# Mixer weights split once inside two feed-forward stages and kept in DRAM, and rotary tables built in the third

## The chip, the cores and the metric

The kernel runs on one core of one Trainium2 chip. The metric is the device time in microseconds (us) of one execution; lower is better. Five engines work side by side: PE (TensorE, matrix products), DVE (VectorE), ACT (ScalarE), POOL (GpSimd) and SP (SyncE, which here only issues transfers). Each takes its own instructions in order and waits for others by semaphores. Transfers between DRAM and the on-chip memory run on 16 shared DMA engines.

## What is computed

A two-layer decoder trunk on 512 tokens of width 1024, all in float32. Each layer is a feed-forward with half weight, a mixer, and a second feed-forward with half weight, each behind an RMS norm and added to the residual. The first layer's mixer is a short gated convolution beside an RWKV-7 recurrence; the second's is a latent attention (MLA) with rotary position encoding. Cut from the reference:

```python
def _swiglu(h, w_gate, w_up, w_down):
    return (jax.nn.silu(h @ w_gate) * (h @ w_up)) @ w_down
...
def _conv_rwkv_mixer(h, w_in, conv_w, mu_shift, w0, w_up, a0, a_up, g_up,
                     k_k, k_a, r_k, ln_w, ln_b, w_out):
...
    p = h @ w_in
    p_conv, p_rwkv = p[..., :3 * CONV_WIDTH], p[..., 3 * CONV_WIDTH:]
...
    y_conv = gate_b * _short_conv(gate_c * h_in, conv_w)
...
    y = _rwkv7_scan(r_h, decay_h, k_h, v_h, -kk, kk * a_h)
...
    return jnp.concatenate([y_conv, y_rwkv], axis=-1) @ w_out
...
def _mla_mixer(h, cos, sin, w_in, q_a_norm, kv_a_norm, w_q_up, w_kv_up, q_norm, k_norm, w_out):
...
    c_q, c_kv, k_pe = jnp.split(p, (Q_RANK, Q_RANK + KV_RANK), axis=-1)
    q = (_rmsnorm(c_q, q_a_norm) @ w_q_up).reshape(B, T, MLA_HEADS, QK_DIM)
    kv = (_rmsnorm(c_kv, kv_a_norm) @ w_kv_up).reshape(B, T, MLA_HEADS, NOPE_DIM + V_DIM)
...
    q = jnp.concatenate([q[..., :NOPE_DIM], _rope(q[..., NOPE_DIM:], cos, sin)], axis=-1)
...
    o = _causal_attention(q, k, v)
    return o.reshape(B, T, MLA_HEADS * V_DIM) @ w_out
```

## The kernel before

The order of the stages is: first feed-forward (ffn 0), convolution and RWKV-7 mixer (`even`), second feed-forward (ffn 1), third feed-forward (ffn 2), latent attention (`mla`), fourth feed-forward (ffn 3). The activations `x` stay on chip as eight tiles of 128 x 512.

**Every product is done as three.** A float32 operand is cut into a high part, a copy rounded to the engine's faster format, and a low part, the remainder. `mm3` (L101 to L105) then multiplies high by high, high by low and low by high. The activations are cut once per stage (`xh`, `xl`, L120 and L121). The weights are cut each time they are used, in `weight` (L67 to L79): a transfer on SP brings a raw block of 128 x 512 (L72, tile `wr`, four buffers), ACT copies it into `wh` (L74), and DVE subtracts to get `wl` (L75); `wh` and `wl` have four buffers each. A caller may hand in `lo_on` to have POOL do the subtraction: the mixer does so for 64 of its 67 blocks (from `proj` and `proj_steps` at L731, the convolution's steps `even_conv` at L1029 and the output product `even_out` at L1081), and the attention's output product `mla_out` (L348) does so for all 16. The attention's input product `mla_in` (L364 to L374) cuts its own 16 blocks into the resident tiles `wih` and `wil`, with every second pair of subtractions on POOL.

**The feed-forward** (`ffn`, L161 to L192) runs 22 gate and up steps, each of two weights of 128 x 1024 (four blocks, 48 matrix instructions), with a SiLU and its own cut of the result behind them (L176 to L184), and then 8 down steps of 66 matrix instructions. Its argument `aside` is called once, in step 2: ffn 0 loads constants there, and ffn 2 builds the rotary tables (`rope_tables`: some forty small DVE instructions of 128 x 128, L244 to L300, and two sines on ACT), with their temporaries in a pool of their own.

**The mixer** interleaves the recurrence's long chains on DVE and ACT with products of the convolution as filler: `fill(n)` takes n steps of the generator `even_conv`, each one `mm3`.

**The order.** The program is written as one stream, and the framework's scheduler then orders each engine's instructions by a simulation of its own, under the dependencies and the buffers' reuse. So the tables of ffn 2 stand, in the order that results, already at the end of `even` and the start of ffn 1, where DVE has their turn. Transfers go round robin over eight slots, so that at most eight of SP's are under way.

## Time and profile before

| | us |
|---|---|
| median of 3 runs | 2032.48 (2031.89 to 2035.05) |
| profiled execution, its own time | 2034.76 |
| its span in the trace | 2032.8 |
| ffn 0 after its first step (24.4 to 373.0) | 348.60 |
| mixer (373.0 to 716.3) | 343.30 |
| ffn 1, first step (716.3 to 732.2) | 15.90 |
| ffn 1, the rest (732.2 to 1080.9) | 348.70 |
| ffn 2 (1080.9 to 1441.6) | 360.70 |
| latent attention (1441.6 to 1668.6) | 227.00 |
| ffn 3, first step (1668.6 to 1680.3) | 11.70 |
| ffn 3, the rest (1680.3 to 2032.0) | 351.70 |

The stretches are cut where PE begins the stage. A row of windows gives the length of a stretch and, for each engine, the microseconds in which it was busy and its number of instructions; then the granted clock of PE as a share of full speed, the mean busy share of the 16 DMA engines and what they moved. An engine busy for the whole stretch sets its length; where none is, the chain of waits and the rows of the single instructions tell who waited for whom.

### The profile page before, as it was taken

The numbers are of one execution on the slowest core, as the hardware profiler recorded it, in microseconds if no ns is written. First come the engines' busy times: TensorE is split into PE (matmuls) and PEld (weight loads), VectorE is DVE, ScalarE is ACT, GpSimd is POOL, SyncE is SP. The second block draws the span as 40 slices with busy tenths as digits, with TensorE's granted clock in tenths as the row PEclk, the third lists the DMA queues.
The fourth block names the chain that finished last, engine by engine and source line by source line (L and its number), as shares of the span: only waits on it lengthen the run. The fifth ranks groups of instructions, "written<-read, shape, count | busy, mean of one in ns | idle before, by whom it ended". The sixth has DMA issues, their size and how long they took to land.

```text
span 2032.8 us, 26989 instructions
## 1 busy us (share of the span) xinstructions
PE 1953.0 (96%) x10030; PEld 1593.5 (78%) x10030; DVE 1083.8 (53%) x1914; ACT 771.1 (38%) x1497; POOL 297.9 (15%) x342
## 2 busy tenths in 40 slices
PE   8999999967999999999999999999988999999999
PEld 6888888756776778888888888888877788888887
DVE  6444433599944874444335444433377775444422
ACT  5333333632422453333333333333475554333321
POOL 2000000266324410000000000000353430000000
PEclk9999999988999999999999999999998999999999
DMA  4222233221111123233333323333311123323332
GB/s 147 95 98 99 91 102 96 78 63 53 47 38 50 60 92 100 94 98 97 96 94 100 97 94 101 94 101 97 96 35 34 42 68 100 98 94 100 102 112 81
DMA packets 99892, 174.47 MB, mean 86 GB/s; under 512 B 11792, under 2 KB 20496, under 8 KB 99760
## 3 DMA queue, kind: packets, MB, share of 16 engines
q1 hardware_dynamic: 99760, 172.74, 27.3%
q8 instruction: 79, 1.29, 0.3%
q14 instruction: 53, 0.43, 0.1%
HBM read 170.60 MB, written 2.10 MB: 85 GB/s over the span
## 4 chain that ended last, share of the span: by engine, by line
PE 65%; DVE 9%; issue 2%; POOL 2%; ACT 2%; DMA 1%; POOLq 0%; ACTq 0%; DVEq 0%
PE po L103 7%; PE po L104 7%; PE po L105 7%; PE pu L103 6%; PE pu L104 6%; PE pu L105 6%; PE pg L104 6%; PE pg L103 6%; PE pg L105 6%; PE pp L103 1%; PE pp L104 1%; PE pp L105 1%; PE s L910 0%; DVE pr L935 0%; DVE ma L942 0%
## 5 line engine op out<-in xcount | busy, mean ns | idle before, releaser
L74 ACT ACTIVATE wh<-wr 128x512 fp32r<-128x512 f32 (+2 forms) x647 | 399.1, 619 | 905.2 <-PE pg L104 455.4
L75 DVE TENSOR_TENSOR wl<-wr,wh 128x512 fp32r<-128x512 f32 (+2 forms) x567 | 384.7, 682 | 413.9 <-ACT wh L74 413.3
L103 PE MATMUL pg<-xh,wh 128*128 128x512 f32 x704 | 276.8, 393 | 6.7 <-ACT wh L74 6.0
L103 PE MATMUL pu<-xh,wh 128*128 128x512 f32 x704 | 275.3, 391 | 3.3 <-DVE x L1088 2.6
L104 PE MATMUL pg<-xl,wh 128*128 128x512 f32 x704 | 275.5, 391 | 1.8 <-DVE xl L121 1.7
L105 PE MATMUL pg<-xh,wl 128*128 128x512 f32 x704 | 274.8, 390 | 0.0
L104 PE MATMUL pu<-xl,wh 128*128 128x512 f32 x704 | 274.8, 390 | 0.0
L105 PE MATMUL pu<-xh,wl 128*128 128x512 f32 x704 | 274.7, 390 | 0.0
L103 PE MATMUL po<-ah,wh 128*128 128x512 f32 x704 | 273.9, 389 | 0.0
L104 PE MATMUL po<-al,wh 128*128 128x512 f32 x704 | 273.9, 389 | 0.0
L105 PE MATMUL po<-ah,wl 128*128 128x512 f32 x704 | 273.9, 389 | 0.0
L176 DVE TENSOR_TENSOR g<-pg,rinv 128x512 f32<-128x512 f32 x88 | 60.9, 692 | 286.8 <-PE pg L105 286.4
L140 POOL TENSOR_TENSOR acc<-acc,sq 128x512 f32<-128x512 f32 x42 | 57.2, 1361 | 1050.9 <-ACT sq L139 1050.6
L103 PEld LDWEIGHTS pg<-xh,wh 128*128 128x128 f32 x704 | 132.7, 188 | 35.3 <-ACT wh L74 6.0
L104 PEld LDWEIGHTS pg<-xl,wh 128*128 128x128 f32 x704 | 132.7, 188 | 32.2 <-DVE xl L121 4.1
L103 PEld LDWEIGHTS pu<-xh,wh 128*128 128x128 f32 x704 | 132.6, 188 | 32.1 <-ACT sin L285 2.9
L105 PEld LDWEIGHTS pu<-xh,wl 128*128 128x128 f32 x704 | 132.6, 188 | 28.0 <-DVE wl L75 0.2
L105 PEld LDWEIGHTS pg<-xh,wl 128*128 128x128 f32 x704 | 132.7, 188 | 27.8 <-DVE wl L75 0.5
L104 PEld LDWEIGHTS pu<-xl,wh 128*128 128x128 f32 x704 | 132.7, 189 | 27.5
L104 PEld LDWEIGHTS po<-al,wh 128*128 128x128 f32 x704 | 132.1, 188 | 27.6
L105 PEld LDWEIGHTS po<-ah,wl 128*128 128x128 f32 x704 | 132.1, 188 | 27.5
L103 PEld LDWEIGHTS po<-ah,wh 128*128 128x128 f32 x704 | 132.1, 188 | 27.2
(365 smaller groups left out, 2641.8 us busy)
## 6 DMA issues: line engine op xcount, KB each, us to landing
wr<-in_wg SPq DMA_DIRECT2D x176, 256.0 KB, 2.5
wr<-in_wu SPq DMA_DIRECT2D x176, 256.0 KB, 2.8
wr<-in_wd SPq DMA_DIRECT2D x160, 256.0 KB, 2.6
wr<-in_w_ei SPq DMA_DIRECT2D x49, 256.0 KB, 2.6
wr<-in_wd SPq DMA_DIRECT2D x32, 128.0 KB, 2.0
wr<-in_w_eo SPq DMA_DIRECT2D x16, 256.0 KB, 2.5
wr<-in_w_oo SPq DMA_DIRECT2D x16, 256.0 KB, 3.0
wr<-in_w_q SPq DMA_DIRECT2D x12, 192.0 KB, 2.4
```

The lines of the kernel that those rows point to most:

```text
L74: nc.scalar.activation(hi, raw, AF.Copy)
L75: (lo_on or nc.vector).tensor_tensor(lo, raw, hi, op=ALU.subtract)
L103: nc.tensor.matmul(ps, wh, xh, start=first, stop=False)
L104: nc.tensor.matmul(ps, wh, xl, start=False, stop=False)
L105: nc.tensor.matmul(ps, wl, xh, start=False, stop=last)
L140: nc.gpsimd.tensor_tensor(acc, acc, sq, op=ALU.add)
L176: nc.vector.tensor_tensor(g, pg, rinv, op=ALU.mult)
```

## The change

In ffn 0 and ffn 1 a new generator, `presplit`, runs beside the gate, up and down steps. It takes the mixer's 67 blocks (17.43 MB, `even_blocks`) in ffn 0 and the attention's 52 blocks (11.53 MB, `mla_blocks`) in ffn 1, in 24 groups, one group per step from step 2 on. A block is loaded (tile `sr`, L113), copied by ACT into `sh` and subtracted by DVE into `sl` one step later, and both parts are sent to DRAM tiles `pre` (L100) a step after that. `weight` then no longer splits such a block: it issues two transfers, of the high part into `wh` (L77) and of the low part into `wl` (L78). `mla_in` does the same for `wih` and `wil` (L428). All POOL subtractions of weights are gone with it. The temporaries of the rotary tables are now in ffn 2's own pool. The on-chip area set aside for the program's DMA descriptors is set to 2048.

```diff
@@ -66,9 +68,15 @@
 
     def weight(self, src, cols, scale=None, lo_on=None):
         nc = self.nc
-        raw = self.wp.tile([128, WCOL], F32, name=self.uid("wr"), tag="wr", bufs=NRAW)[:, 0:cols]
+        raw = None
+        if not isinstance(src, tuple):
+            raw = self.wp.tile([128, WCOL], F32, name=self.uid("wr"), tag="wr", bufs=NRAW)[:, 0:cols]
         hi = self.wp.tile([128, WCOL], F32R, name=self.uid("wh"), tag="wh", bufs=NSPLIT)[:, 0:cols]
         lo = self.wp.tile([128, WCOL], F32R, name=self.uid("wl"), tag="wl", bufs=NSPLIT)[:, 0:cols]
+        if isinstance(src, tuple):
+            nc.sync.dma_start(hi.bitcast(F32), src[0])
+            nc.sync.dma_start(lo.bitcast(F32), src[1])
+            return hi, lo
         nc.sync.dma_start(raw, src)
         if scale is None:
             nc.scalar.activation(hi, raw, AF.Copy)
@@ -78,6 +86,34 @@
             nc.vector.scalar_tensor_tensor(lo, raw, scale, hi, op0=ALU.mult, op1=ALU.subtract)
         return hi, lo
 
+    def presplit(self, pool, groups):
...
+        nc = self.nc
+        tile_ = lambda tag, n, dt: pool.tile([128, WCOL], dt, name=self.uid(tag), tag=tag, bufs=6)[:, 0:n]
+        loaded, ready = [], []
+        for group in chain(groups, ((), ())):
+            for key, hi, lo in ready:
+                both = []
+                for a in (hi, lo):
+                    dst = self.dp.tile([128, a.shape[-1]], F32, name=self.uid("pre"))
+                    nc.sync.dma_start(dst, a.bitcast(F32))
+                    both.append(dst)
+                self.pre[key] = tuple(both)
+            ready = []
+            for key, raw in loaded:
+                n = raw.shape[-1]
+                hi, lo = tile_("sh", n, F32R), tile_("sl", n, F32R)
+                nc.scalar.activation(hi, raw, AF.Copy)
+                nc.vector.tensor_tensor(lo, raw, hi, op=ALU.subtract)
+                ready.append((key, hi, lo))
+            loaded = []
+            for key, src in group:
+                raw = tile_("sr", src.shape[-1], F32)
+                nc.sync.dma_start(raw, src)
+                loaded.append((key, raw))
+            yield
+
...
-    def ffn(self, j, y=None, aside=None):
+    def ffn(self, j, y=None, aside=None, later=()):
         tc, nc = self.tc, self.nc
+        later = list(later)
...
+            steps = NF + KD - 6 if later else 0
+            n = len(later)
+            split = self.presplit(ap, [later[n * i // steps : n * (i + 1) // steps] for i in range(steps)])
             for m in range(NF):
+                if m > 1:
+                    next(split, None)
...
                 if m == 2 and aside is not None:
-                    aside()
+                    aside(ap)
...
             for m in range(KD):
+                next(split, None)
...
-    def rope_tables(self, mp):
-        with self.tc.tile_pool(name="rope", bufs=1) as rp:
-            self.rope_build(rp, mp)
-
-    def rope_build(self, rp, mp):
-        nc = self.nc
-        t = lambda s: rp.tile([128, 4, 32], F32, name=self.uid(s))
-        pi = rp.tile([128, 4], mybir.dt.int32, name="posi")
+    def rope_tables(self, mp, ap):
+        nc = self.nc
+        a = ap.tile([128, 8 * T], F32, name="ropetmp", tag="ropetmp")
+        free = [a[:, i * 128 : i * 128 + 128] for i in range(28)]
+        t = lambda s: free.pop().rearrange("p (b f) -> p b f", b=4)
+        pi = ap.tile([128, 4], mybir.dt.int32, name="posi")
...
-        gn = rp.tile([128, 128], F32, name="gn")
+        gn = free.pop()
         nc.sync.dma_start(gn, self.d["rope_g"])
-        ng = rp.tile([128, 256], F32, name="ng")
+        ng = a[:, 28 * 128 : 30 * 128]
         nc.sync.dma_start(ng, self.d["nope_g"])
...
+    def mla_blocks(self):
+        d, out = self.d, []
+        for k in range(KD):
+            for c in (slice(0, 384), slice(384, 704)):
+                out.append((("w_oi", k, c.start), d["w_oi"][k][:, c]))
+        for hp in range(4):
+            for k in range(2):
+                out.append((("w_kv", hp, k), d["w_kv"][hp, :, k * 512 : k * 512 + 512]))
+            for k in range(3):
+                out.append((("w_q", hp, k), d["w_q"][hp, :, k * 384 : k * 384 + 384]))
+            for m in range(0, KD, 2):
+                out.append((("w_oo", hp, m), d["w_oo"][hp, :, m * 256 : m * 256 + 512]))
+        return out
...
         for m in range(0, KD, 2):
-            wh, wl = self.weight(self.d["w_oo"][hp, :, m * 256 : m * 256 + 512], 512, lo_on=nc.gpsimd)
+            wh, wl = self.weight(self.pre["w_oo", hp, m], 512)
...
             for c in (slice(0, 384), slice(384, 704)):
-                raw = self.wp.tile([128, WCOL], F32, name=self.uid("wr"), tag="wr", bufs=NRAW)[:, 0 : c.stop - c.start]
-                nc.sync.dma_start(raw, d["w_oi"][k][:, c])
-                nc.scalar.activation(h[:, c], raw, AF.Copy)
-                (nc.vector if k % 2 == 0 else nc.gpsimd).tensor_tensor(l[:, c], raw, h[:, c], op=ALU.subtract)
+                for dst, src in zip((h, l), self.pre["w_oi", k, c.start]):
+                    nc.sync.dma_start(dst[:, c].bitcast(F32), src)
...
     def mla_proj(self, hp, t):
         d, nc = self.d, self.nc
-        wk = [self.weight(d["w_kv"][hp, :, k * 512 : k * 512 + 512], 512) for k in range(2)]
+        wk = [self.weight(self.pre["w_kv", hp, k], 512) for k in range(2)]
...
-        wq = [self.weight(d["w_q"][hp, :, k * 384 : k * 384 + 384], 384) for k in range(3)]
+        wq = [self.weight(self.pre["w_q", hp, k], 384) for k in range(3)]
...
+    def even_blocks(self):
+        w, out = self.d["w_ei"], []
+        for col, m in [(0, 64), (64, 96)] + [(160 + i * 128, 128) for i in range(24)]:
+            step = min(KD, WCOL // m) * m
+            for a in range(0, KD * m, step):
+                out.append((("w_ei", col * 8 + a), w[:, col * 8 + a : col * 8 + min(KD * m, a + step)]))
+        for half in range(2):
+            for m in range(KD):
+                out.append((("w_eo", m, half), self.d["w_eo"][m, :, half * 512 : half * 512 + 512]))
+        return out
...
-    def proj_steps(self, col, m, lo_on=None):
+    def proj_steps(self, col, m):
         ps = self.mm.tile([128, T], F32, name=self.uid("pp"), tag="mm")
-        yield from self.gemm_steps([(ps[0:m], self.d["w_ei"][:, col * 8 : col * 8 + 8 * m])], KD, m, self.xh, self.xl, lo_on)
+        yield from self.gemm_steps([(ps[0:m], lambda a, b: self.pre["w_ei", col * 8 + a])], KD, m, self.xh, self.xl)
         return ps[0:m]
...
         k = rw["MB"][j][:, 0:4].rearrange("p c t -> p (c t)")
-        self.shiftmix(self.proj(160 + j * 128, 128, nc.gpsimd), MU_K + j, k)
+        self.shiftmix(self.proj(160 + j * 128, 128), MU_K + j, k)
...
             po = self.mm.tile([128, T], F32, name=self.uid("po"), tag="mm")
             h = slice(half * 4, half * 4 + 4)
-            src = self.d["w_eo"][m, :, half * 512 : half * 512 + 512]
-            yield from self.gemm_steps([(po, src)], 4, 128, self.oh[h], self.ol[h], nc.gpsimd)
+            src = lambda a, b: self.pre["w_eo", m, half]
+            yield from self.gemm_steps([(po, src)], 4, 128, self.oh[h], self.ol[h])
...
     with ExitStack() as st:
         k = Even(tc, d, st)
         k.norm(0)
-        k.ffn(0, aside=k.mla_setup)
+        k.ffn(0, aside=k.mla_setup, later=k.even_blocks())
         k.even(1)
         k.norm(2)
-        k.ffn(1)
+        k.ffn(1, later=k.mla_blocks())
         k.norm(3)
         with tc.tile_pool(name="ropec", bufs=1) as rp:
-            k.ffn(2, aside=lambda: k.rope_tables(rp))
+            k.ffn(2, aside=lambda ap: k.rope_tables(rp, ap))
             k.mla(4)
         k.norm(5)
...
-    nc = bacc.Bacc("TRN2", target_bir_lowering=False, num_devices=1)
+    nc = bacc.Bacc("TRN2", target_bir_lowering=False, num_devices=1, dynamic_dma_scratch_size=2048)
```

**POOL in the mixer.** What stands in a row on POOL where the decay of the recurrence begins (L816 to L818 before, L881 to L883 after; `y` and `lv` are decay tiles, `wl` the low part of a weight). Before:

```order
L75 TENSOR_TENSOR wl_3176<-wr_3174,wh_3175 128x512
L75 TENSOR_TENSOR wl_3212<-wr_3210,wh_3211 128x512
L75 TENSOR_TENSOR wl_3230<-wr_3228,wh_3229 128x512
L816 COPY lc<-y_2896 128x8
L818 TENSOR_TENSOR e_3200<-y_2896,lv 128x512
L739 MEMSET q_3246 128x1
L75 TENSOR_TENSOR wl_3283<-wr_3281,wh_3282 128x512
L75 TENSOR_TENSOR wl_3301<-wr_3299,wh_3300 128x512
L816 COPY lc<-y_2897 128x8
L75 TENSOR_TENSOR wl_3354<-wr_3352,wh_3353 128x512
L818 TENSOR_TENSOR e_3271<-y_2897,lv 128x512
```

After:

```order
L881 COPY lc<-y_3568 128x8
L883 TENSOR_TENSOR e_3858<-y_3568,lv 128x512
L804 MEMSET q_3900 128x1
L881 COPY lc<-y_3569 128x8
L883 TENSOR_TENSOR e_3925<-y_3569,lv 128x512
L804 MEMSET q_3967 128x1
L881 COPY lc<-y_3570 128x8
L883 TENSOR_TENSOR e_3992<-y_3570,lv 128x512
L804 MEMSET q_4034 128x1
L881 COPY lc<-y_3571 128x8
L883 TENSOR_TENSOR e_4059<-y_3571,lv 128x512
```

The subtractions `wl<-wr,wh` (64 on POOL in the mixer) have left POOL; of the rest the order is the same.

**SP in ffn 0.** The transfers of some gate and up steps in the steady part. Before:

```order
L72 DMA wr_1198<-in_wu 128x512
L72 DMA wr_1228<-in_wg 128x512
L72 DMA wr_1234<-in_wu 128x512
L72 DMA wr_1276<-in_wg 128x512
L72 DMA wr_1282<-in_wu 128x512
```

After:

```order
L80 DMA wr_680<-in_wg 128x512
L80 DMA wr_686<-in_wu 128x512
L100 DMA pre_874<-sh_774 128x512
L100 DMA pre_876<-sl_775 128x512
L100 DMA pre_878<-sh_778 128x512
L100 DMA pre_880<-sl_779 128x512
L100 DMA pre_882<-sh_782 128x512
L80 DMA wr_716<-in_wg 128x512
L100 DMA pre_884<-sl_783 128x512
L80 DMA wr_722<-in_wu 128x512
L113 DMA sr_894<-in_w_ei 128x512
L113 DMA sr_896<-in_w_ei 128x512
```

Between the weights of the feed-forward (`wr`) there are now the raw loads of the mixer's blocks (`sr`) and the two stores of each (`pre`), in the one queue of SP.

**SP from ffn 2 to the attention.** The transfers around the last down step of ffn 2 and the attention's input weights (L372 before, L428 after). Before:

```order
L72 DMA wr_11670<-in_wd 128x512
L72 DMA wr_11688<-in_wd 128x256
L372 DMA wr_11717<-in_w_oi 128x384
L372 DMA wr_11721<-in_w_oi 128x320
L372 DMA wr_11727<-in_w_oi 128x384
L372 DMA wr_11731<-in_w_oi 128x320
```

After:

```order
L80 DMA wr_15435<-in_wg 128x512
L80 DMA wr_15441<-in_wu 128x512
L77 DMA wh_13117<-pre_7812 128x512
L78 DMA wl_13118<-pre_7814 128x512
L77 DMA wh_13121<-pre_7912 128x512
L78 DMA wl_13122<-pre_7914 128x512
L77 DMA wh_13349<-pre_7916 128x384
L78 DMA wl_13350<-pre_7918 128x384
L77 DMA wh_13353<-pre_8016 128x384
L428 DMA wih_12742<-pre_7070 128x384
L428 DMA wil_12743<-pre_7072 128x384
L428 DMA wih_12742<-pre_7074 128x320
```

The first four weights of ffn 3, two key-value blocks and one and a half query blocks now stand ahead of the input weights `wih` and `wil`; all 32 transfers of the latter follow, where before raw loads of the input weights directly followed the last down weight.

## Rows read from the trace of the kernel before

**Rows 1.** The page, first part: busy us (share of the span), instructions.

```profile
PE 1953.0 (96%) x10030; PEld 1593.5 (78%) x10030; DVE 1083.8 (53%) x1914; ACT 771.1 (38%) x1497; POOL 297.9 (15%) x342
```

**Rows 2.** Windows by stage: us, busy us of each engine, PEclk, DMA share, GB/s.

```profile
24.40:373.00 348.60, 348.60 (x1538) 288.43 (x1537) 154.36 (x239) 118.41 (x193) 7.81 (x6) 1.00 0.32 98
373.00:716.30 343.30, 300.15 (x2555) 227.88 (x2554) 263.33 (x485) 135.61 (x258) 151.26 (x143) 0.95 0.18 54
716.30:732.20 15.90, 13.28 (x49) 10.37 (x50) 14.28 (x21) 10.34 (x18) 5.82 (x4) 0.89 0.25 85
1441.60:1668.60 227.00, 205.75 (x1132) 172.78 (x1133) 160.82 (x421) 136.10 (x427) 99.75 (x161) 0.98 0.18 55
1668.60:1680.30 11.70, 11.69 (x51) 9.02 (x50) 11.56 (x14) 6.62 (x12) 5.87 (x4) 1.00 0.18 56
```

**Rows 3.** Windows inside the even mixer, same columns.

```profile
393.00:413.00 20.00, 15.93 (x61) 11.87 (x60) 12.42 (x34) 18.98 (x35) 6.96 (x8) 0.91 0.17 48
413.00:500.00 87.00, 63.87 (x380) 49.15 (x378) 83.02 (x124) 24.39 (x39) 55.73 (x56) 0.89 0.20 58
500.00:566.00 66.00, 58.44 (x709) 46.91 (x711) 62.35 (x86) 27.80 (x59) 22.71 (x24) 0.94 0.16 46
566.00:660.00 94.00, 91.60 (x1124) 67.10 (x1117) 43.23 (x122) 26.45 (x59) 33.16 (x26) 0.98 0.14 44
660.00:716.30 56.30, 50.74 (x213) 39.39 (x214) 48.76 (x102) 24.97 (x51) 24.79 (x22) 1.00 0.19 60
```

**Rows 4.** Groups by line, even mixer: busy us, mean ns, then idle.

```profile
L75 POOL TENSOR_TENSOR wl<-wr,wh 128x512 fp32r<-128x512 f32 x64 | 86.4, 1355 | 111.3 <-ACT wh L74 94.0 <-PE pp L105 13.1 <-PE po L103 1.5
...
L74 ACT ACTIVATE wh<-wr 128x512 fp32r<-128x512 f32 x65 | 40.3, 624 | 89.9 <-PE pp L104 72.9 <-issue 14.3 <-PE po L104 1.6
...
L806 ACT ACT_TABLE_LOAD x1 | 1.3, 1283 | 0.0
```

**Rows 5.** Timeline of DVE and POOL: start us, us, engine, line.

```profile
407.96 1.79 DVE L819 SCALAR_TENSOR_TENSOR lv<-e,lv 128x512 f32<-128x512 f32 x1 [0.57 <-POOL q L739]
...
442.99 0.75 DVE L1045 SCALAR_TENSOR_TENSOR k<-u,ev,k 128x512 f32<-128x512 f32 x1 [0.24 <-ACT k L1044]
...
445.37 1.77 DVE L1046 SCALAR_TENSOR_TENSOR k<-u,ev,k 128x512 f32<-128x512 f32 x1
...
443.55 3.04 POOL L75 TENSOR_TENSOR wl<-wr,wh 128x512 fp32r<-128x512 f32 x2 [1.35 <-PE pp L105]
...
710.22 1.31 DVE L257 TENSOR_SCALAR dg<-rest 128x128 f32<-128x128 f32 x1
```

**Rows 6.** Line L801 alone: ns min/median/max, first and last start.

```profile
L801 DVE TENSOR_TENSOR_SCAN y<-y,zero x32: 256/264/1380, 404.3 to 432.6; 128x64 f32<-128x64 f32 x32
```

**Rows 7.** Chain of waits near 436 us: start us, us, what.

```profile
436.28 1.27 POOL wl L75
```

**Rows 8.** Groups by line, first feed-forward from 24.4 to 373 us.

```profile
L75 DVE TENSOR_TENSOR wl<-wr,wh 128x512 fp32r<-128x512 f32 (+2 forms) x133 | 89.3, 674 | 102.5 <-ACT wh L74 102.5
L74 ACT ACTIVATE wh<-wr 128x512 fp32r<-128x512 f32 x132 | 81.5, 618 | 196.8 <-PE pg L104 110.4 <-PE po L104 66.1 <-issue 7.1
```

**Rows 9.** DMA view of 0 to 24.4 us, in 40 slices; the page's DMA issues.

```profile
GB/s 0 0 11 73 222 356 292 238 185 161 285 282 316 349 400 400 410 403 406 410 400 282 121 57 0 0 84 299 319 256 114 8 0 0 0 0 0 0 0 27
...
wr<-in_wg SPq DMA_DIRECT2D x176, 256.0 KB, 2.5
```

**Rows 10.** Timeline of DVE near 717 us; waits from 716 to 720 us.

```profile
717.00 1.32 DVE L278 TENSOR_SCALAR rnd<-hs 128x128 f32<-128x128 f32 x1
...
PE pu L103 <- DVE x L1088: 2.6, 1, 2.6
```

**Rows 11.** Windows of the latent attention: its start, and the rest.

```profile
1441.60:1461.60 20.00, 19.77 (x119) 18.75 (x120) 7.84 (x15) 10.30 (x22) 10.48 (x10) 1.00 0.59 182
1461.60:1668.60 207.00, 185.98 (x1015) 154.02 (x1014) 152.98 (x406) 125.80 (x406) 89.27 (x151) 0.98 0.14 43
```

**Rows 12.** Groups by line, latent attention, POOL.

```profile
L75 POOL TENSOR_TENSOR wl<-wr,wh 128x512 fp32r<-128x512 f32 x16 | 20.9, 1308 | 35.9 <-ACT wh L74 35.9
```

More of the change, by code (lines that the diff above doesn't have):

```diff
@@ L43, in __init__ @@
         self.sm = open_(name="sm", bufs=4, space=PSUM)
+        self.dp = open_(name="presplit", bufs=1, space=bass.MemoryType.DRAM)
+        self.pre = {}
         self.n = 0
@@ L89, in gemm_steps @@
             k1 = min(nk, k0 + step)
-            w = [self.weight(src[:, k0 * m : k1 * m], (k1 - k0) * m, lo_on=lo_on) for _, src in outs]
+            cut = lambda src: src(k0 * m, k1 * m) if callable(src) else src[:, k0 * m : k1 * m]
+            w = [self.weight(cut(src), (k1 - k0) * m, lo_on=lo_on) for _, src in outs]
             for k in range(k0, k1):
@@ L205, with mla_setup @@
 class Mla(Trunk):
-    def mla_setup(self):
+    def mla_setup(self, _):
         nc, cp = self.nc, self.cp
@@ L721, in v, with proj @@
         return self.ev[0:p, base + j : base + j + 1]
-    def proj(self, col, m, lo_on=None):
-        g = self.proj_steps(col, m, lo_on)
+    def proj(self, col, m):
+        g = self.proj_steps(col, m)
         while True:
@@ L1035, in even_conv @@
             col = 160 + 1536 + j * 384
-            pc = yield from self.proj_steps(col, 128, nc.gpsimd)
+            pc = yield from self.proj_steps(col, 128)
             cs = self.g(("k", "a", "n", "w")[j])
             nc.scalar.activation(cs, pc, AF.Copy)
-            ph = yield from self.proj_steps(col + 128, 128, nc.gpsimd)
+            ph = yield from self.proj_steps(col + 128, 128)
             u = self.t("u", 514)
@@ L1047, in even_conv @@
             nc.gpsimd.tensor_tensor(cs, cs, self.rv, op=ALU.mult)
-            pb = yield from self.proj_steps(col + 256, 128, nc.gpsimd)
+            pb = yield from self.proj_steps(col + 256, 128)
             nc.vector.tensor_tensor(cs, pb, cs, op=ALU.mult)
```

8 lines of the change are left out of this document (4 added, 4 removed).

## The prediction

> **What bounds the kernel now.** I read the page's busy times first: PE is busy for 96% of the span [rows 1]. That is a mean over stages with different limits, so the windows by stage come next [rows 2]. In ffn 0 after its first step PE is busy for 348.60 of 348.60 us at full clock, DVE for 154.36, ACT for 118.41; ffn 1 to ffn 3 read the same. Nothing can be won there, only lost: this is where the change puts its new work. The mixer is different: in 343.30 us PE works 300.15, DVE 263.33 and POOL 151.26. The attention leaves 21 us of PE idle (227.00 less 205.75), and the first step of ffn 1 lasts 15.90 us against 11.70 for the same step of ffn 3.
>
> The windows inside the mixer tell which engine sets the pace [rows 3]. From 393 to 413 us it is ACT (18.98 of 20.00). From 413 to 566 us it is DVE: 83.02 of 87.00 and then 62.35 of 66.00 us, while PE has 63.87 and 58.44. From 566 to 660 us PE is busy for 91.60 of 94.00, so little is to be had. From 660 to 716.3 us PE has 50.74 and DVE 48.76 of 56.30, handing work to each other.
>
> What slows DVE there is seen in the timeline. The same kind of instruction, 128 x 512 with three operands, takes 0.75 us at 442.99 and 1.77 us at 445.37, beside a pair of weight subtractions on POOL from 443.55 to 446.59 [rows 5]. The 64-column scans of L801 have a median of 264 ns and a maximum of 1380 ns [rows 6]. POOL's 64 subtractions in the mixer take 86.4 us [rows 4]. Of all DVE instructions of the mixer that lie beside one of them, 40 are longer than the median of their own form, from the one at 407.96 to the one at 710.22 [rows 5]; the excess, each less its median, adds up to 36.9 us: 1.1 before 408, 22.6 (23 instructions) from 408 to 566, 2.5 to 660, and 10.7 after that.
>
> **The mixer: what is removed.** All 64 POOL subtractions and 65 ACT copies go. Between 408 and 566 us DVE sets the time, so the 22.6 us of stretch come off the path, less what the next limit keeps. PE's own idle time in these two windows is 23.13 and 7.56 us, so PE would not stop a gain of 22.6; but the recurrence's hand-overs and POOL's other operations (L816 to L896), which stretch DVE too, stay. I take −20, with −12 and −25 as ends. POOL's subtraction is also a link of the chain itself, as at 436.28 us for 1.27 us [rows 7]; it is one of a few there, and −1 more.
>
> From 393 to 413 us ACT bounds. Six weight copies at 624 ns [rows 4] are 3.7 us of it, but the order of the changed kernel has two more activation table loads there, at 1283 ns each [rows 4]: net −1, ends −4 and +2. From 566 to 660 us at most 2.4 us of idle PE can vanish: −1. From 660 to 716.3 us PE idles for 5.56 us, which caps the gain although the stretch is 10.7 us: −3, ends 0 and −5. **Sum for the mixer −26, ends −15 and −36.**
>
> What is added to the mixer: two transfers of 256 KB for each block in place of one, so about 108 GB/s where 54 are moved [rows 2]; 256 KB land 2.5 us after issue [rows 9], and a block's buffer comes free three blocks of products (12 matrix instructions each) ahead of its use. I cost that at nothing; if the cover fails, each block that comes late costs up to those 2.5 us, less the split of 1.3 us (0.62 on ACT and 0.67 on DVE [rows 8]) that no longer stands behind it.
>
> **The head of ffn 1.** The rotary tables leave DVE's turn. At 717.00 us one of their instructions takes 1.32 us, and PE waits 2.6 us for the residual addition (L1088) behind it [rows 10]. At best the step falls to ffn 3's 11.70: −4.2. But the order puts some eight splits of the attention's blocks into this same stretch, at 0.67 us of DVE and 0.62 of ACT each; DVE is already busy 14.28 of the 15.90 us. I take −3, ends −4 and +2. In ffn 2 the forty table instructions of about 0.3 us meet a DVE that is busy for less than half (as 154.36 of 348.60 [rows 2]): 0 to +0.5; without that cover they would cost some 12 us.
>
> **Ffn 0 and ffn 1: what is added.** Engines: 67 copies at 618 ns and 67 subtractions at 674 ns [rows 8] in about 21 steps, so 3.2 of each per step. A gate and up step lasts 10.88 us (48 products 0.2265 us apart). DVE has eight instructions in it now, 5.5 us; with 2.2 more 7.7. ACT has 3.7 of copies and SiLU and goes to below 6. Both fit, and their waits are one step old, so PE stays full: 0 to +1.
>
> Transfers: from the changed order, 57.4 MB lie between the sixth and the thirty-eighth pair of weights on SP's queue, which is 16 steps: 3.59 MB per step, where it was 1.05. Over 10.88 us this is 330 GB/s. What the queue can give is bounded by two rows. In the load at the start the stream holds 400 to 410 GB/s for several slices of 0.6 us, with 256 KB transfers [rows 9]. Going by share, 98 GB/s at 0.32 give 306 and 54 at 0.18 give 300 [rows 2]. I take the first, since it is a measured rate, while the share at a light load also counts packets that wait; so the stream fits with a fifth to spare. What queues behind a late store on SP is the next weight load; that has been issued some 8 us before its split. **Sum +1; at 300 GB/s +35, see the first rival.**
>
> The Trainium skill, on the page "SBUF — State Buffer", section "The DMA setup-cost knee", puts a 256 KiB transfer at 224 GB/s, and the section after it says that two concurrent ones serialize. By that, a step would need 16 us and the kernel would stand near 2170 us. The 400 GB/s with the same size of transfer speak against it [rows 9]; I leave it 0.01 of the first rival's chance below.
>
> **The attention.** It gains in the middle: POOL's 20.9 us of subtractions in `weight` go [rows 12], as do 22 on DVE and the copies on ACT. But PE is busy for 185.98 of the 207.00 us after the start [rows 11], and only eight DVE instructions are stretched there, by 5.6 us together: −6, ends −14 and 0. It loses at the start. There PE is busy for 19.77 of 20.00 us now [rows 11], since raw input weights wait in buffers. In the changed order the input weights stand behind a load into a `wh` buffer that the last product of ffn 2 releases. So the first arrives one landing (2.5 us) and two or three issues later: PE idles 3.5 us. After that, 0.72 MB for each 128 rows come in 1.8 us at 400 GB/s, about as fast as PE uses them. So +3.5, ends +2 and +8. The third part of each of four query weights has its buffer late; two landings replace a split: +0.5, ends 0 and +6. **Sum −2, ends −12 and +12.**
>
> **The sum.** −26 −3 +1 +0.5 −2 is about −30. On the profiled execution's own 2034.76 us (span 2032.8 and 2.0 outside it) this gives 2005, and on the median of 2032.48 us, 2.3 lower, about 2002.5: I say 2003.
>
> **Rivals.**
> 1. *Transfers become the bound of ffn 0 and ffn 1.* If reading and writing together give 300 GB/s, a step's 3.59 MB take 11.97 us, 1.09 more than PE; over 21 steps of ffn 0 and 11 of ffn 1 this is +35, and the time is 2038. It begins below 330 GB/s and turns the change into a loss of over 4 us below some 299. For it: the rates by share, and that no row shows stores beside loads. Against: 400 to 410 GB/s. 0.13.
> 2. *The stretch hides other waits.* POOL's other operations run earlier and hit DVE as often, or the chain's hand-overs take the gain; the mixer gains 10 and the time is 2019. For it: "issue" and ACT links lie between the DVE pieces. Against: DVE busy 95% of its windows. 0.17.
> 3. *The splits were hidden anyway.* The mixer keeps its length, the head of ffn 1 gains 3 and the attention loses 2: 2032. Against: the link at 436.28. 0.07.
> 4. *The attention's start is worse.* The 32 transfers delay its first weights and the next ones at each step: +10 in place of −2, 2015. 0.08.
> 5. *More is won.* All of the mixer's stretch and chain links (−36), and the attention −8: 1987. 0.05.
>
> **How the numbers follow.** The forecast has 0.50. A measurement of this kernel can tell 0.2%, about 4 us, from no change. Faster by more than that are the forecast and rivals 2, 4 and 5: 0.80. Rival 3 is the same: 0.07. Rival 1 is slower: 0.13. The range leaves out rival 1 and the edge of rival 5, and holds the milder form of rival 1 (304 to 330 GB/s, up to +30): 1987 to 2034.
>
> **What would show it.** In the profile after: no weight subtraction on POOL; scans of L801's kind near 264 ns except beside other POOL work; the mixer about 317 us, DVE still the busiest up to 566; the first step of ffn 1 near 12.9; PE without gaps in ffn 0 and ffn 1 at some 330 GB/s; an idle PE of 3.5 us at the attention's start, and the attention at 225. I am wrong if PE waits for `wr` splits in the gate and up steps (rival 1), if the mixer's DVE windows stay near 153 us with less busy time (rival 2), or if PE waits for transfers inside the mixer.

## The result: faster, by three quarters of the forecast

The changed kernel takes 2011.14 us in the median of four runs (2007.84 to 2014.93), against 2032.94 before (now four runs in place of three): a ratio of 0.9892 (0.9870 to 0.9914), 21.8 us. The forecast was 2003, a gain of 29.5. The profiled execution took 2013.32 us, with a span of 2011.5, so the two spans differ by 21.3 us. Cut at the first matrix instruction of each stage, they divide as follows.

| stage | before | after | measured | forecast |
|---|---|---|---|---|
| ffn 0 | 367.03 | 377.38 | +10.4 | 0 to +1 |
| mixer | 343.27 | 312.13 | −31.1 | −26 |
| ffn 1, first step | 15.94 | 11.34 | −4.6 | −3 |
| ffn 1, the rest | 348.60 | 354.76 | +6.2 | in the +1 |
| ffn 2, with PE's idle time at the attention's entry | 360.71 | 364.55 | +3.8 | +0.5 and +3.5 |
| latent attention | 227.05 | 221.19 | −5.9 | −5.5 |
| before ffn 0, and ffn 3 | 370.17 | 370.19 | 0.0 | 0 |

So the mixer gained more than forecast, and the two feed-forward stages gave 16.6 us back where 1 had been set down.

The windows of the changed kernel (columns as in [rows 2]): the steady part of ffn 0, the mixer, the first and the third step of ffn 1, the end of that third step alone, the steps behind it, and the start of the attention.

```profile
60.00:264.00 204.00, 201.12 (x867) 161.15 (x867) 125.42 (x202) 95.11 (x166) 0.00 (x0) 1.00 0.92 315
383.30:695.40 312.10, 293.73 (x2556) 226.29 (x2555) 223.31 (x468) 107.92 (x207) 68.35 (x81) 0.97 0.38 123
695.40:706.70 11.30, 11.30 (x51) 9.19 (x50) 10.20 (x14) 6.86 (x14) 2.78 (x2) 1.00 0.76 242
718.50:734.60 16.10, 13.75 (x49) 9.93 (x50) 11.42 (x20) 8.35 (x17) 0.00 (x0) 0.89 0.91 297
729.50:732.30 2.80, 2.80 (x8) 2.21 (x7) 2.02 (x5) 1.45 (x3) 0.00 (x0) 0.50 1.02 361
734.60:800.00 65.40, 65.40 (x290) 54.17 (x289) 41.29 (x68) 30.91 (x55) 0.00 (x0) 1.00 0.95 319
1426.00:1446.00 20.00, 19.97 (x118) 20.00 (x119) 0.27 (x2) 0.78 (x3) 1.40 (x2) 0.93 0.86 280
```

Against [rows 2]: in the mixer POOL falls from 151.26 us to 68.35, DVE from 263.33 to 223.31, ACT from 135.61 to 107.92, and PE's idle time from 43.2 to 18.4. In ffn 0 PE issues 867 matrix instructions in 204 us, where 0.2265 us each would be 196.4; DVE and ACT have room, and the DMA engines are busy for 92% at 315 GB/s. The scans, which answer [rows 6], have lost their tail:

```profile
L866 DVE TENSOR_TENSOR_SCAN y<-y,zero x32: 261/266/288, 414.9 to 434.3; 128x64 f32<-128x64 f32 x32
```

Where ffn 0 waits is seen in the groups by line from 60 to 264 us (busy us, mean ns | idle time before it and what ended it) and in the DMA issues of the same stretch, to be laid beside [rows 8] and the last row of [rows 9]:

```profile
L83 DVE TENSOR_TENSOR wl<-wr,wh 128x512 fp32r<-128x512 f32 x73 | 48.4, 682 | 0.2 <-ACT wh L82 0.2
L82 ACT ACTIVATE wh<-wr 128x512 fp32r<-128x512 f32 x74 | 42.4, 618 | 5.0 <-PE pg L141 4.4 <-ACT wh L82 0.4
L108 DVE TENSOR_TENSOR sl<-sr,sh 128x512 fp32r<-128x512 f32 x56 | 37.9, 690 | 72.4 <-ACT sh L107 72.3
L107 ACT ACTIVATE sh<-sr 128x512 fp32r<-128x512 f32 x56 | 35.1, 631 | 91.2 <-DMA sr<-in_w_ei 66.6 <-DMA sr<-in_w_eo 24.1
```

```profile
pre<-sh SPq DMA_DIRECT2D x57, 256.0 KB, 5.5
...
sr<-in_w_ei SPq DMA_DIRECT2D x38, 256.0 KB, 5.4
wr<-in_wg SPq DMA_DIRECT2D x33, 256.0 KB, 4.6
```

A transfer that landed 2.5 us after its issue takes about 5 now, and ACT stands for 91.2 of the 204 us in front of a copy `sh` whose raw block has not landed. What that does to PE is seen at 178 to 180 us, in the timelines of ACT and of PE (start us, us, then idle time and its releaser):

```profile
172.32 1.66 ACT L82 ACTIVATE wh<-wr 128x512 fp32r<-128x512 f32 x3
178.49 0.63 ACT L107 ACTIVATE sh<-sr 128x512 fp32r<-128x512 f32 x1 [4.52 <-DMA sr<-in_w_ei]
179.03 0.62 ACT L222 ACTIVATE g<-g 128x512 f32<-128x512 f32 x1
179.55 0.61 ACT L82 ACTIVATE wh<-wr 128x512 fp32r<-128x512 f32 x1
```

```profile
180.22 0.50 PE L140 MATMUL pu<-xh,wh 128*128 128x512 f32 x1 [0.43 <-ACT wh L82]
```

The weight copy at 179.55 had its data: by the order of loads and copies, its block had landed at 172.40 us. It stood behind the SiLU, and that behind the copy `sh`. PE then waits for it. The third step of ffn 1 (16.08 us for 10.88) has the same order of events: ACT idles 4.05 us in front of `sh`, and PE 1.55 us in front of `wh`. Part of the 5.2 us lost there comes after the wait: from 729.5 to 732.3 us PE does not idle, but its granted clock is 0.50, the lower of its two levels (1.2 GHz), and its products come 0.43 us apart in place of 0.23.

### The profile page after: what moved, and what is told of

It is laid out like the page before. It is cut to its first block, busy times and chain, and to the rows that moved or that the text cites. A ratio compares the mean times of both kernels' runs of the same rounds, so it can differ in the third digit from the quotient of the medians.

```text
span 2011.5 us, 27586 instructions
## 1 busy us (share of the span) xinstructions
PE 1955.8 (97%) x10030; PEld 1591.9 (79%) x10030; DVE 1082.2 (54%) x2002; ACT 765.5 (38%) x1498; POOL 180.9 (9%) x254
## 4 chain that ended last, share of the span: by engine, by line
PE 80%; DVE 7%; DMA 6%; ACT 2%; issue 2%; SPq 1%; POOL 1%; DVEq 0%; ACTq 0%; POOLq 0%
PE po L140 9%; PE po L142 9%; PE po L141 9%; PE pu L142 6%; PE pg L141 6%; PE pg L142 6%; PE pu L140 6%; PE pg L140 6%; PE pu L141 6%; DMA sr<-in_w_ei 2%; PE pp L140 2%; PE pp L141 2%; PE pp L142 2%; DMA pre<-sh 2%; DMA wr<-in_wu 1%
## 5 line engine op out<-in xcount | busy, mean ns | idle before, releaser
L82 ACT ACTIVATE wh<-wr 128x512 fp32r<-128x512 f32 (+1 forms) x544 | 330.0, 616 | 626.0 <-PE pg L141 290.1
L83 DVE TENSOR_TENSOR wl<-wr,wh 128x512 fp32r<-128x512 f32 (+1 forms) x544 | 365.1, 677 | 359.4 <-ACT wh L82 359.3
```

The lines of the kernel that those rows point to most:

```text
L82: nc.scalar.activation(hi, raw, AF.Copy)
L83: (lo_on or nc.vector).tensor_tensor(lo, raw, hi, op=ALU.subtract)
```

## Experiments

All ratios are to the kernel before, run beside the variant. Each theory goes by the letter that its expectation gives it.

**The stores left out.** Is it the transfers' rate?

```diff
+                n = hi.shape[-1]
+                if n in self.kept:
+                    self.pre[key] = self.kept[n]
+                    continue
...
-                self.pre[key] = tuple(both)
+                self.pre[key] = self.kept[n] = tuple(both)
```

> The changed kernel, with its loads, copies and subtractions in ffn 0 and ffn 1 as they are, but only the first block of each width is stored to DRAM; every later use reads that block's parts, so the weights of the mixer and the attention are wrong and the transfers as many and as large as before there. A gate and up step moves about 1.9 MB in place of 3.6. Theory A (the transfers' rate of about 312 GB/s bounds ffn 0): the steps of ffn 0 fall back to 10.88 us and the first gate and up part from 257.7 to about 247.5 us, that of ffn 1 from 246.4 to about 241; the kernel gains 13 to 16 us on the changed one. Theory B (the added copies and subtractions delay the weight splits on ACT and DVE): ffn 0 stays near 257 us and the gain is under 4 us.

0.9882 (0.9862 to 0.9902): 2011.39 us, no faster than the changed kernel. Ffn 0 lasts 375.5 us in place of 377.4. By the numbers this is theory B (the gate and up part takes 255.8 us, the gain is under 4). But the edit changed more than the stores: with them gone the scheduler moved the loads forward, and the time is lost in the first 120 us alone, which the windows show:

```profile
45.00:100.00 55.00, 52.98 (x225) 42.62 (x224) 48.33 (x79) 38.70 (x69) 0.00 (x0) 0.97 0.90 289
100.00:150.00 50.00, 49.12 (x211) 38.90 (x210) 34.06 (x55) 25.42 (x44) 0.00 (x0) 1.00 0.54 169
150.00:250.00 100.00, 100.00 (x443) 82.84 (x442) 46.46 (x72) 33.18 (x54) 0.00 (x0) 1.00 0.31 99
```

From 45 to 100 us PE issues 225 instructions for a possible 243, at 289 GB/s, less than the 315 of the changed kernel; where the blocks are all split, it loses nothing. The loss goes with the blocks' splits, and it is not undone by fewer bytes in all. Since loads and splits now come in a shorter time, it does not decide cleanly between the theories.

**Raw blocks in the rotation of the weights.** The same bytes, paced.

```diff
-NRAW = 4
+NRAW = 8
...
-                raw = tile_("sr", src.shape[-1], F32)
+                n = src.shape[-1]
+                raw = self.wp.tile([128, WCOL], F32, name=self.uid("wr"), tag="wr", bufs=NRAW)[:, 0:n]
```

> The changed kernel, with the raw blocks of the mixers taken from the same rotation of buffers as the feed-forward's raw weights (now eight), so that a raw load can no longer run ahead of the step in whose place the program has it. The same bytes in all, but 3.3 MB in place of 3.6 per gate and up step of ffn 0 and about 2.4 in ffn 1. Theory A: 3.3 MB at 312 GB/s are 10.6 us, under the 10.88 of PE: most of the 10.4 us lost in ffn 0 and of the 6 in ffn 1 come back, the kernel gains 8 to 14 us on the changed one. Theory B: the same copies and subtractions, so no gain; a rotation shared with the weights may even cost some us.

0.9927 (0.9906 to 0.9948): slower than the changed kernel, by 10 us in the medians and 7 by the two ratios. Ffn 1 came out clean (359.94 us), as theory A has it; but ffn 0 grew to 389.7, with the DMA engines at only 83% and 272 GB/s:

```profile
60.00:264.00 204.00, 191.56 (x805) 149.65 (x804) 111.05 (x180) 83.77 (x148) 0.00 (x0) 0.99 0.83 272
```

ACT's timeline in it:

```profile
109.75 1.28 ACT L107 ACTIVATE sh<-wr 128x512 fp32r<-128x512 f32 x2 [6.05 <-DMA wr<-in_w_ei]
...
122.56 1.32 ACT L107 ACTIVATE sh<-wr 128x512 fp32r<-128x512 f32 x2 [6.15 <-DMA wr<-in_w_ei]
```

A rate that is not reached can't be the bound. ACT stands for 6 us at a time in front of a copy whose block is still under way. This gave theory G: the place of the copies in ACT's order is what costs.

**The copies queued behind their step.** Theory G tested with the same bytes:

```diff
-                nc.scalar.activation(hi, raw, AF.Copy)
-                nc.vector.tensor_tensor(lo, raw, hi, op=ALU.subtract)
+                self.tc.keep_in_program_order(nc.scalar.activation(hi, raw, AF.Copy))
+                self.tc.keep_in_program_order(nc.vector.tensor_tensor(lo, raw, hi, op=ALU.subtract))
```

> The changed kernel, with each copy and subtraction of a mixer's block queued, on ACT and on DVE, behind what the program has ahead of it: a block that was loaded in one step is copied after the SiLU and the cut of that step, so over a step after its load was issued. The bytes are the same, about 3.2 MB per gate and up step in ffn 0 (the variant with the shared rotation had 3.3) and 2.4 in ffn 1. Theory G (ACT, in order, stood at copies whose loads had not landed, with the next weights' copies behind them): ffn 0 falls from 377.4 to about 367.5 us, ffn 1 from 366.1 to about 360, the kernel is 13 to 16 us faster than the changed one, near 1996. Theory A (the rate of the transfers): as for the shared rotation, which had the same rate, ffn 0 loses 8 us or more against the kernel before.

0.9819 (0.9801 to 0.9837): 1998.97 us, with runs from 1993.3 to 2000.4; the profile is of the fastest. Ffn 0 is 366.95 us and ffn 1 359.94; each step but the first two lasts 10.88 again. The window of ffn 0 and ACT's timeline there:

```profile
60.00:247.00 187.00, 187.00 (x827) 154.88 (x826) 115.51 (x187) 88.72 (x155) 0.00 (x0) 1.00 0.88 299
```

```profile
154.50 1.31 ACT L82 ACTIVATE wh<-wr 128x512 fp32r<-128x512 f32 x2 [4.12 <-DMA wr<-in_wg]
155.71 0.62 ACT L222 ACTIVATE g<-g 128x512 f32<-128x512 f32 x1
157.80 0.63 ACT L226 ACTIVATE ah<-u 128x512 fp32r<-128x512 f32 x1 [1.47 <-DVE u L223]
158.34 1.66 ACT L107 ACTIVATE sh<-sr 128x512 fp32r<-128x512 f32 x3
```

The three copies now follow the step's own work without a wait, at 299 GB/s, a higher rate than the 272 at which the shared rotation lost 22.7 us. Theory G holds: the gain on the changed kernel is 12 us in the medians and 15 by the two ratios, for 13 to 16. The order held also spreads the load: 3.2 MB per step in place of the changed kernel's 3.59; but the shared rotation had 3.3 and lost.

**The same, in 18 groups.** Is there a rate that bounds as well?

```diff
-            steps = NF + KD - 6 if later else 0
+            steps = NF - 4 if later else 0
```

> As the one with the queued copies, but the mixer's blocks in 18 groups in place of 24, so that about 4.0 MB per step stand on SP's queue in ffn 0 (372 GB/s at 10.88 us) and about 3.1 in ffn 1 (285). Theory A in its remaining form (the transfers have a rate of their own that bounds above some 312 to 345 GB/s): the 17 steps of ffn 0 take 11.7 to 12.9 us each, ffn 0 is 14 to 34 us longer than with 24 groups, while ffn 1 stays clean. Theory G alone: a load of 372 GB/s fits under the 400 of the start, and ffn 0 stays within 3 us of the one with 24 groups.

0.9989 (0.9980 to 0.9998): 2032.01 us, all but 2.4 us of the gain lost again. Ffn 0 lasts 399.1 us, ffn 1 stays at 359.94. Ordered as in the last variant, with 4.0 MB per step, the transfers reach a mean of 311 GB/s (first row); the other rows are three single steps:

```profile
60.00:260.00 200.00, 182.65 (x762) 145.50 (x761) 116.17 (x185) 87.12 (x153) 0.00 (x0) 0.96 0.91 311
79.48:96.86 17.38, 11.88 (x50) 8.60 (x48) 10.15 (x17) 8.00 (x15) 0.00 (x0) 0.94 0.92 304
96.86:110.21 13.35, 13.35 (x48) 10.45 (x49) 4.19 (x8) 3.43 (x7) 0.00 (x0) 0.83 0.85 294
121.09:131.97 10.88, 10.88 (x49) 9.01 (x48) 7.58 (x13) 5.14 (x9) 0.00 (x0) 1.00 1.03 366
```

The 32.1 us lost lie in the range of theory A's remaining form, but its picture does not: the steps do not take 11.7 to 12.9 us each. Of the 19 behind the first two, eight stay at 10.88, one of them at 366 GB/s. Three of 17.3 to 17.4 us, each with one of 12.7 to 13.4 behind it, make up 26 of the 32.1 us; in the second of such a pair PE is busy throughout, at a granted clock of 0.83. What SP itself waits for from 60 to 260 us names another cause (us, times, longest):

```profile
SPq L113 <- DVE sl L108: 15.4, 24, 2.7
```

The raw loads wait for a free buffer `sr`: six must hold two groups, now of up to four blocks each, and the next weights stand behind them on SP. With 24 groups, of at most three, the same view has no such wait. So there are two candidates, the rate and the six buffers, and no run with more buffers divides them. An estimate by share: 311 GB/s at 0.91 would be 342 with the engines full, at which 4.04 MB take 11.8 us, so the rate alone would explain some 16 of the 32 us.

**Both parts of a block in one store.** What sets the 311?

```diff
-                both = []
-                for a in (hi, lo):
-                    dst = self.dp.tile([128, a.shape[-1]], F32, name=self.uid("pre"))
-                    nc.sync.dma_start(dst, a.bitcast(F32))
-                    both.append(dst)
-                self.pre[key] = tuple(both)
+                dst = self.dp.tile([128, 2, hi.shape[-1]], F32, name=self.uid("pre"))
+                nc.sync.dma_start(dst, lo.bitcast(F32))
+                self.pre[key] = (dst[:, 0, :], dst[:, 1, :])
...
+                pair = pool.tile([128, 2, WCOL], F32R, name=self.uid("sh"), tag="sh", bufs=6)[:, :, 0:n]
+                hi, lo = pair[:, 0, :], pair[:, 1, :]
...
+                ready.append((key, hi, pair))
```

(At the store, `lo` is the tile of both parts.)

> As the one with 18 groups, with both parts of a block in one tile and stored by one transfer of 512 KB in rows of 4 KB, in place of two of 256 KB in rows of 2 KB; the bytes per step are the same, 4.0 MB. Theory N (the 310 GB/s that 18 groups reached are set by the number of packets or transfers, of which a sixth to a third are now saved): ffn 0 falls from 399 by 8 us or more, and the rate in its steady part rises above 330 GB/s. Theory O (the bytes, or stores beside loads, set it): ffn 0 stays within 4 us of 399 and the rate at 300 to 320.

1.0006 (0.9997 to 1.0015): ffn 0 is 404.0 us, 4.9 longer, and the rate is 299 GB/s with engines less busy:

```profile
60.00:260.00 200.00, 178.67 (x731) 142.41 (x730) 112.39 (x179) 85.07 (x151) 0.00 (x0) 0.94 0.84 299
```

Theory N's forecast (8 us less, over 330 GB/s) did not come, and theory O's band (within 4 us of 399, 300 to 320 GB/s) was just missed as well. But the engines are idle for 16% here, and SP's raw loads wait for a buffer three times as long as with two stores:

```profile
SPq L111 <- DVE sh L106: 50.5, 23, 7.3
```

So the edit did not test N: something else than the packets held the transfers up. What sets the rate, the bytes, the stores beside loads, the round of eight slots or the buffers, is open.

**The mixer's subtractions on DVE.** The kernel before, with one edit, asks where the mixer's gain is from.

```diff
-            w = [self.weight(src[:, k0 * m : k1 * m], (k1 - k0) * m, lo_on=lo_on) for _, src in outs]
+            w = [self.weight(src[:, k0 * m : k1 * m], (k1 - k0) * m) for _, src in outs]
```

> The kernel before, with the mixer's 64 weight subtractions on DVE and none on POOL; nothing is stored, nothing moved. Theory C (what the mixer gained is the DVE time that POOL's subtractions had stretched): from 408 to 566 us 31 subtractions of 0.67 us, 21 us, take the place of 22.6 us of stretch, so the mixer stays at 343 us, within 5, and the kernel is the same within 6 us. Theory D (the mixer gained since the products no longer wait for POOL's subtractions, a link of 1.3 us that 0.7 on DVE would shorten as well): the mixer is 10 us shorter or more.

0.9938 (0.9923 to 0.9953): 2023.44 us; the mixer lasts 332.7 us, 10.5 less. By the time this is theory D, though most of C's account of DVE is borne out: with 50.9 us of subtractions added, DVE's busy time in the mixer only went from 263.33 to 266.52. Added up one by one, DVE's instructions in the mixer other than weight subtractions last 288.0 us before and 247.0 here; 4.9 of these 41.0 us are nine table instructions that now fall behind the mixer. So POOL's subtractions had stretched DVE's work by 36 us, as the prediction's 36.9 had it. (The windows' busy time can't be used for this difference: records of one engine overlap a little, and a window counts such time once.)

```profile
373.30:706.00 332.70, 302.22 (x2555) 229.01 (x2554) 266.52 (x541) 138.05 (x259) 72.14 (x80) 0.94 0.19 56
```

```profile
L75 DVE TENSOR_TENSOR wl<-wr,wh 128x512 fp32r<-128x512 f32 x65 | 50.9, 789 | 12.3 <-ACT wh L74 11.7 <-PE pp L105 0.2 <-issue 0.2
```

A third of the mixer's gain needs nothing stored: POOL took 1355 ns for what DVE does in 789, and cost DVE 36 us to save it 51. D's mechanism is not shown, however. The idle time of PE in front of products that wait for `wl` grew, from 2.0 us to 13.9. From the waits in the mixer (us, times, longest), before:

```profile
PE s L859 <- DVE sv L887: 10.1, 3, 6.9
PE s L859 <- DVE b L844: 9.3, 4, 4.2
PE s L829 <- ACT sq L827: 9.3, 1, 9.3
...
PE pp L105 <- POOL wl L75: 2.0, 1, 2.0
```

In this variant:

```profile
PE pp L105 <- DVE wl L75: 13.9, 4, 5.3
PE s L859 <- DVE b L844: 4.5, 2, 4.0
```

What shrank are PE's waits for the recurrence: in front of L829, L859 and L1069 it idled for 33.8 us before and for 6.3 here. The scheduler also ordered the mixer anew, and on POOL the recurrence's own instructions no longer stand in a row with subtractions; which of these the 10.5 us are was not tested.

**Only the low parts kept.** On the variant "first rows" below, the mixer's high parts are copied by ACT from the raw block again.

```diff
-            nc.sync.dma_start(hi.bitcast(F32), src[0])
+            if keep:
+                nc.sync.dma_start(raw, src[0])
+                nc.scalar.activation(hi, raw, AF.Copy)
...
-                for a in (hi, lo):
+                for a in (hi, lo)[key[0][:3] in ("w_e",) :]:
```

> As the one with the first rows in buffers of their own, but of the mixer's blocks only the low part is kept in DRAM; in the mixer a block's raw form is loaded again and ACT copies it into the high part, as in the kernel before. One store less per block in ffn 0 (2.5 MB per step in place of 3.2), 65 ACT copies back in the mixer, no subtraction on DVE or POOL there. Theory L (in the mixer the subtractions' place on DVE and POOL was what cost): the mixer stays within 3 us of 311. Theory M (the copies on ACT hold products up as well, in 393 to 413 us above all, where ACT set the pace): the mixer is 317 us or longer. Ffn 0 stays at 367 by either.

0.9797 (0.9780 to 0.9813), 1991.55 us, as without it (1991.58). The mixer lasts 310.0 us in place of 311.5, with 33.6 us more on ACT:

```profile
373.40:683.40 310.00, 289.84 (x2555) 221.88 (x2554) 220.43 (x464) 140.36 (x265) 68.66 (x82) 0.98 0.38 119
```

Theory L: the copies were hidden. From the 332.7 us with all subtractions on DVE to these 310.0, what is left but for 1.9 us of the tables (below) goes, by remainder, to the subtractions that leave DVE.

**The tables moved, nothing else,** on the kernel before.

```diff
...
-            k.ffn(2, aside=lambda: k.rope_tables(rp))
+            k.ffn(2, aside=lambda ap: k.rope_tables(rp, ap))
```

> The kernel before, with the rotary tables' temporaries in ffn 2's pool as in the changed kernel, and nothing else. Theory E (the tables on DVE held up the head of ffn 1): the first step of ffn 1 falls from 15.94 to 11.3 us as in the changed kernel, the end of the mixer by 1 to 3, ffn 2 stays: 4 to 8 us faster. Theory F (the head was held up by the stretched subtractions on POOL in the mixer's tail): the first step stays above 14 us and the kernel is the same within 2 us.

0.9971 (0.9958 to 0.9984): 5.7 us faster. The first step of ffn 1 is 11.34 us as in the changed kernel (15.94 before), the mixer 1.9 shorter, ffn 2's steps unchanged (240.3 us for gate and up in both). Theory E. Ffn 2's down steps came out 1.4 us longer and the attention 1.5; why was not looked into.

**The attention's weights split in place,** the mixer's kept in DRAM.

```diff
...
-            k.ffn(1, later=k.mla_blocks())
+            k.ffn(1)
```

> The changed kernel with the attention's weights split in place as before; only the first mixer's blocks are kept in DRAM, and the tables are moved. Theory H (the attention's part gains 6 us in the attention and gives back 6 in ffn 1 and 3 at the attention's entry): ffn 1 is 360, ffn 2 about 361, the attention 227 to 228.5, and the kernel is the same as the changed one within 5 us, or up to 4 faster. Theory I (the attention's part pays): the kernel is 6 us or more slower than the changed one.

0.9894 (0.9878 to 0.9911), the same as the changed kernel. Ffn 1 is 359.94 us (366.10 there), ffn 2 362.08 (364.55), the attention 228.90 (221.19): what the attention's part won it gave back, 8.6 against 7.7 us. Theory H.

**First rows.** On the variant with the queued copies, the attention's first 128 input rows have buffers of their own:

```diff
+        self.win0 = [cp.tile([128, 704], F32R, name=f"{n}0") for n in ("wih", "wil")]
...
-            h = iw.tile([128, 704], F32R, name=f"wih{k}")
-            l = iw.tile([128, 704], F32R, name=f"wil{k}")
+            h, l = self.win0 if k == 0 else [iw.tile([128, 704], F32R, name=f"{n}{k}") for n in ("wih", "wil")]
```

> As the one with the queued copies, with the input weights of the attention's first 128 rows (high and low) in buffers of their own, which are free long before, so that their loads need not wait for the end of ffn 2. Theory J (the 3.1 us that PE idles at the attention's start are the landing of these weights): the idle time falls by the 1.9 us of products that the first rows feed, ffn 2's last part from 124.3 to about 122, and the kernel is 2 to 3 us faster than with the queued copies alone. Theory K (the following rows come late in their turn): the idle time moves behind the first rows, gain under 1 us.

0.9788 (0.9773 to 0.9802): 1991.58 us, the fastest beside the two variants built on it. Ffn 2 lasts 361.3 us in place of 364.5. In the windows of the attention's start PE works 19.08 of 20.00 us, where it had 19.97 behind an idle 3.1:

```profile
1405.90:1425.90 20.00, 19.08 (x119) 18.50 (x118) 1.61 (x3) 1.63 (x3) 2.31 (x2) 1.00 0.88 290
```

Some 0.9 us of the wait moved behind the first rows (theory K in part), the rest is gone (J): ffn 2 and the attention together are 2.5 us shorter than with the queued copies alone.

**More blocks in the down steps,** on the last variant.

```diff
-            steps = NF + KD - 6 if later else 0
-            n = len(later)
-            split = self.presplit(ap, [later[n * i // steps : n * (i + 1) // steps] for i in range(steps)])
+            at = [sum((1, 2)[j >= NF - 2] for j in range(i)) for i in range(NF + KD - 3)] if later else [0]
+            at = [len(later) * a // max(at[-1], 1) for a in at]
+            split = self.presplit(ap, [later[a:b] for a, b in zip(at, at[1:])])
```

> As the one with the first rows in buffers of their own, with a down step (15 us) given twice as many blocks as a gate and up step (10.9 us): 2.6 MB per gate and up step of ffn 0 in place of 3.2, 241 GB/s. Theory P (at 300 GB/s the queued copies are still near the limit, and their runs lie from 1993 to 2000 us for it): the time is at or under the 1991.6 us of the one before it, and its runs lie within 2 us. Theory Q (nothing is left there): the same within 1 us, the spread too.

0.9797 (0.9783 to 0.9812), 1992.42 us. At 244 GB/s in ffn 0 in place of 299 nothing more is won, and the runs lie as close as before (1991.1 to 1992.6 against 1990.9 to 1992.2): theory Q. Why the variant with the queued copies alone spread from 1993.3 to 2000.4 stays open.

## Why the prediction came out as it did

**The mixer: right in what is removed, too small in what it is worth.** The mixer gained 31.1 us for 26, inside the stated ends of 15 and 36. Cut at the first matrix instruction of a line (lines of the kernel before): up to that of L783 it gained 0.6 us; from there to that of L953, the stretch that ACT and DVE bound, 25.4 (forecast 22 with the −1 for ACT); to that of L1064 it lost 1.4 (forecast a gain of 1); and the tail gained 6.6 (forecast 3). The size of the stretch was read rightly, 36.9 us for the 36 that the variant with the subtractions on DVE shows. But the step from it to the time was too simple. Given back to DVE, the subtractions ate more than the freed time, and 10.5 us were still won; with them gone from DVE as well, the stretch up to L953 gained more than the 22.6 us of stretched instructions in it. PE's waits for the recurrence shrank by more than that; by which link is open. The link for which I set down −1 from a single row [rows 7], POOL's subtraction ahead of PE, is not shown to be the source: PE's products waited for it for 2.0 us in all. Of the transfers added to the mixer, costed at nothing, no cost is seen: at 123 GB/s the waits there list none of PE for a transfer.

**Ffn 0 and ffn 1: wrong, +16.6 for +1.** One step is shown to have failed, a second is likely. The first is "Both fit, and their waits are one step old, so PE stays full". I added busy times and never asked where the copies would stand in ACT's order. In the order that the scheduler's simulation made, ACT reached the copies before their blocks had landed, and the SiLU and the next weight's copy stood behind them. With the order held, the loss was gone at once (377.4 to 366.95 and 366.1 to 359.94). The second is "I take the first, since it is a measured rate": 400 to 410 GB/s were the rate of a few microseconds of loads. The mix of loads and stores had means of 299 to 319 GB/s over 65 us and more, at shares of 0.88 to 0.95, which by share is 336 to 342 with full engines (an estimate). The 330 GB/s that a step asks for would just fit, with next to nothing and not a fifth to spare; the 300 to 306 of the light load were too low, as the 400 was too high. By this estimate the changed kernel's 3.59 MB take 10.5 to 10.7 us, still under PE's 10.88, which makes the order the larger part; no run divides the two. That 3.59 MB at the measured 315 GB/s give 11.4 us proves nothing: it is the measured time over again. Of the first rival, the stage and the sign came true, PE waiting for the splits of `wr`; its +35 did not, and its cause, the rate, is not what the runs show first. The range held its milder form.

**The head of ffn 1: right.** It gained 4.6 for 3, from the tables alone, as the variant with nothing else shows. The splits that took their place in DVE's turn cost it nothing.

**The attention: right by its parts.** Entry +3.8 with what ffn 2 lost elsewhere (+3.5 and +0.5), the rest −5.9 (−6 and +0.5). The link is the one named: SP's timeline in the changed kernel shows the last load into `wh` leaving at 1422.75 us, while the last products of ffn 2 run, and the input weights right behind it.

```profile
1422.75 0.32 SPq L77 DMA_DIRECT2D wh<-pre  x1
1423.16 0.38 SPq L428 DMA_DIRECT2D wih<-pre  x1
```

```profile
1426.03 0.66 PE L457 MATMUL pab<-wih,xh 128*128 128x384 f32 x1 [3.08 <-issue]
```

**Rivals.** Of the second (the mixer gains 10 only), the third (nothing gained) and the fourth (the entry worse) nothing is seen. The forecast was 8 us too low: the feed-forward's part, priced without the order and at the most favourable rate, cost 15.6 us more than set down, and the mixer and the head of ffn 1 gave 6.7 more than set down. That the two errors went against each other was luck.

## What to carry to other kernels

An engine with half of its time free can still be the one that holds PE up: of added work on an in-order queue, ask at which place in the order it stands, what it waits for there, and what needed work is behind it, before adding up busy times. Give a copy that waits for a transfer a place behind the work of its own step, a full step after the load's issue. Take a transfer rate from a stretch as long and as mixed as the one that is planned. Before a lower rate is called the bound, look at single steps, and at what the queue that issues the transfers waits for itself: a mean rate is bytes over time, whatever the cause. And before a precomputed operand is stored, try the cheaper edit: a third of the mixer's gain came from having the subtraction on another engine, and the high parts need not have been stored at all.

## What the runs showed of the hardware that was not expected

Loads and stores of 256 KB issued side by side by one engine reached 299 GB/s without any loss to PE (88% share). Over 65 us and more no run had a mean above 319 (95% share), though a single step of 10.9 us had 366 with PE full, and a short burst of loads alone had 400 to 410. The time to land grew more slowly than the rate: for a weight 2.5 us at 98 GB/s, 3.5 to 3.7 at 244, 4.0 to 4.2 at 299, 4.6 to 4.7 at 315. POOL's subtractions, 86.4 us of them, stretched the same DVE work by 36 us over the mixer; almost all of it lies in instructions that are longer by more than 0.2 us each. A wait of PE can cost more than its length: in the variant with 18 groups PE idled for 4.84 us before 96.86, and the step behind it took 13.35 us in place of 10.88, with PE busy throughout at a granted clock of 0.83.
